# Small start loads on SyncE's queue, two expert passes per accumulation, and a rearranged end in a mixture-of-experts decoder layer

## The chip, the cores and the metric

The kernel runs on one core of one Trainium2 chip. The metric is the device time of one execution in microseconds (us); lower is better. Times come from repeated executions of the same program, and one further execution was profiled.

## What is computed

One decoder layer over 512 tokens of width 1024, all in float32: a mixer (four mLSTM heads and eight sliding-window attention heads), a normalisation, a hierarchical mixture of experts, and a second normalisation. Cut to what matters here:

```
p = x @ W_in                                  # 2824 columns, conv + silu on the first 1024
y = W_out [ mLSTM_heads(p) ; SWA_sink_heads(p) ]
x = LN1(alpha * x + y)
g   = argmax(x @ w_group_router + b_group_router)          # one of 4 groups
e   = top-2 of the 8 experts of group g                    # two weights per token
out = sum over the token's two experts of  weight * (silu(x @ gate[e]) * (x @ up[e])) @ down[e]
x = LN2(alpha * x + out)
```

There are 32 experts; gate, up and down of one expert are 1 MiB each, so the experts' weights are 96 MiB, and every one is read once.

## The kernel before, in words

**Start.** Tokens stand in four chunks of 128. SyncE's queue (SP) loads the transposed input in four pieces (`xc`, L159) and `W_in` in column groups (`wraw`, L153; group 0 in thirds). ScalarE (ACT) rounds each piece to a high part (`xh`, `wh`, L185), VectorE (DVE), and for a few pieces GpSimd (POOL), subtracts it to get the low part (`xl`, `wl`, L186), and TensorE (PE) multiplies high by high, low by high and high by low (L234, L235, L239). Before its first real product PE runs ten warm-up products (L654). Group 0 is done for chunks 0 to 3, then groups 1 and 2; their results are copied out of PSUM at L258 to L264 (`tq`, `gates`). The small inputs (gate bias, attention sinks, rope tables cos and sin, conv weights and bias, the mLSTM norm's weights, the two router biases) are loaded through POOL's queue (L167, L686 to L701). POOL also builds the masks and then turns queries and keys (`rope`, L330 to L340).

**Queue order.** SP, PE and DVE run in the order in which the kernel is written wherever `manual_schedule` names them; elsewhere, for ACT and POOL, a scheduler chooses. In the built program each transfer of SP also waits until the one eight places ahead of it has landed, so at most eight are under way.

**Experts.** Thirteen passes (`NP = 13`), their kinds in `ORDER = "BBBCABABABBCC"`. A pass of kind A or B serves two experts, one of kind C four, over 128 gathered rows of tokens. Pass p: POOL gathers the rows (`xg`, L1000), PE transposes them (L1012), `gu_part` multiplies by gate and up in four quarters of 2 of 8 K blocks (L1044; a quarter needs the weights of all experts of the pass, quarters 0 and 1 the first half of each, 2 and 3 the second), `pair_h` makes silu(gate) * up (ACT L1059, DVE L1060), `dn_t` transposes it (PE L1067, DVE copy L1069), `pass_dn` multiplies by down (L1077). `y_split` scales the result and splits it into `yh` (ACT, L1087) and `yl` (DVE, L1088); `back_hot` makes a 0/1 matrix `oh` of the tokens (L1096); and `add_back` brings the result back to the tokens: for every chunk c and half u one accumulation in PSUM, `oh` times `yh` and `oh` times `yl` (L1113), added by DVE to the running rows `x1` (L1115; the first time L1118). In the loop over p the quarters of pass p stand between the pieces of the `add_back` of pass p - 2, the transposes and the down product of pass p - 1. Passes 0 and 1 share one accumulation, every later pass has its own.

Weights lie in 16 ring slots of 1 MiB; `prefetch` issues a load on SP as soon as a slot is free, in the order pass, then first half of gate and up, second half, down (for the last pass the second half of down comes at the very end).

**The end.** After the loop: broadcast rows of the last norm (`l2_fill`, L1461), a matrix of rows that belong to the same token (`same_rows`, L1471), `add_back` of pass 10, down product and `add_back` of pass 11, the norm of every chunk (`norm_s` statistics on DVE L1527, with small steps on POOL L194 to L1531; `norm_i` on ACT L1539; `norm_z` times weight on DVE L1543; `norm_o` plus bias L1546, three halves of eight on POOL and five on DVE; `norm_d` output on SP L1549). Then pass 12 (kind C): quarters 0 and 1 (`last_gu(0)`), `base_rows` of all four chunks (L1562, the running rows of the tokens that this pass serves), quarters 2 and 3 (`last_gu(1)`), `pair_h`, `dn_t`, down, a scaled copy (ACT, DVE L1604), a product with `same` (L1606), a norm of those rows (L1611, L1613) and one scatter over the output (POOL, L1614). A loop over further rows follows; it runs only when experts overflow.

```python
            if prev:
                py = pass_dn(hts[0], p - 1)
                parts = later([(back(p - 1), y_split(py, cws[:, p - 1:p], *y_slots()))])
```

Of the kernel before, what the change touches and what calls it, by code (L numbers as in the profile page):

```python
# [23 lines left out]
NCH = 4  # L24
P = 128
# [47 lines left out]
def ap_of(src, offset, dims):  # L73
    return bass.AP(tensor=src.tensor, offset=src.offset + offset, ap=dims)
# [3 lines left out]
def layer_kernel(ctx, tc, x, w_in, conv_w, conv_b, gate_bias, norm_w, sinks, w_out, ln1_w, ln1_b,  # L78
# [84 lines left out]

    ident = C.tile([P, P], F32, name="ident")
    make_identity(nc, ident)
    def bload(t, src, n):
        G.dma_start(t, ap_of(src, 0, [[0, P], [1, n]]))  # L167
        return t

    gbias = bload(C.tile([P, 8], F32, name="gbias"), gate_bias, 8)  # L170


    def some(g, n):
# [509 lines left out]
        return u  # L683

    sink = bload(C.tile([P, 8], F32, name="sink"), sinks, 8)
    G.dma_start(cosd, cos_t.rearrange("(c p) d -> p c d", p=P))  # L686
    G.dma_start(sind, sin_t.rearrange("(c p) d -> p c d", p=P))
    cw = C.tile([P, 4, 8], F32, name="cw")
    G.dma_start(cw, ap_of(conv_w, 0, [[32, P], [8, 4], [1, 8]]))
    cb = C.tile([P, 8], F32, name="cb")  # L690
    G.dma_start(cb, ap_of(conv_b, 0, [[8, P], [1, 8]]))
    triu = tri("triu", 1, OP.is_ge)
    ktri = tri("ktri", -1, OP.is_ge, I32)
    negm = tri("negm", 1, OP.is_ge, BF16, val=0.0, fill=-1e30)
# [2 lines left out]
    G.tensor_scalar(nw, nw, 0.5, None, op0=OP.mult)  # L697
    rb = C.tile([1, 40], F32, name="rb")
    G.memset(rb, -1e30)
    G.dma_start(rb[:, 0:4], ap_of(b_gr, 0, [[0, 1], [1, 4]]))  # L700
    G.dma_start(rb[:, 8:40], ap_of(b_er, 0, [[0, 1], [1, 32]]))  # L701
    mhalf = C.tile([P, 4], F32, name="mhalf")
    G.memset(mhalf, -0.5)
    iot = C.tile([P, 2 * P], F32, name="iot")
# [358 lines left out]
    def dn_t(h):  # L1063
        ph = bank("ph", tag="t")[:, 0:256].rearrange("p (j n) -> p j n", j=2)
        hv = h.rearrange("p (q j) -> p j q", j=2)
        for j in range(2):
            TE.transpose(ph[:, j], hv[:, j], ident)  # L1067
        ht = W.tile([P, DE], F32, name="ht", bufs=1).rearrange("p (j n) -> p j n", j=2)
        V.tensor_copy(ht, ph)  # L1069
        return ht  # L1070
# [10 lines left out]
    def pass_dn(ht, p):  # L1081
        return dn_mm(ht, pairs[p], TILES[ORDER[p]])

    def y_split(py, cs, yh, yl):
        for u in range(2):
            us = slice(512 * u, 512 * u + 512)
            A.activation(yh[:, us], py[u], AF.Copy, scale=cs)  # L1087
            V.scalar_tensor_tensor(yl[:, us], py[u], cs, yh[:, us], op0=OP.mult, op1=OP.subtract)  # L1088
        return yh, yl

    def y_slots():
        return [slot(n, F32R)[:, :DM] for n in ("yh", "yl")]
# [12 lines left out]
    def add_back(oys, cs=range(NCH)):  # L1105
        mm = [(o, t) for o, y in oys for t in y]
        for c in cs:
            for u in range(2):
                us = slice(512 * u, 512 * u + 512)
                xu = x1[c][:, us]  # L1110
                b = bank("cb", tag="pj")
                for i, (o, t) in enumerate(mm):
                    TE.matmul(b, o[:, c * P:(c + 1) * P], t[:, us], start=i == 0, stop=i == len(mm) - 1)  # L1113
                if (c, u) in scaled:
                    V.tensor_add(xu, xu, b)  # L1115
                else:
                    scaled.add((c, u))
                    V.scalar_tensor_tensor(xu, xu, ALPHA, b, op0=OP.mult, op1=OP.add)  # L1118
# [334 lines left out]
    def l2_fill(i):  # L1453
        d, w = l2d
        t = slot("l2")[:, :DM]
        l2.append(t)
        for u in range(2):
            g = 2 * i + u
            p_ = bank("l2")
            for s in range(2):  # L1460
                TE.matmul(p_, w[:, g:g + 1].to_broadcast([16, P]), d[:, s].rearrange("p k n -> p (k n)"),  # L1461
                          start=s == 0, stop=s == 1)
            A.copy(t[:, 512 * u:512 * u + 512], p_)


    def same_rows(p):
        t = slot("same")
        m, w = t[:, 0:P], t[:, P:2 * P + 2]
        tk = tok2[0][:, p:p + 1]
        b = bank("same", tag="t")  # L1470
        TE.matmul(b[:, 0:P], tk.to_broadcast([P, P]), ident, start=True, stop=True)  # L1471
        V.tensor_scalar(m, b[:, 0:P], tk, None, op0=OP.is_equal)
        V.scalar_tensor_tensor(w[:, 0:P], triu, 0.5, m, op0=OP.is_lt, op1=OP.mult)
        V.tensor_reduce(w[:, P:P + 1], w[:, 0:P], axis=AX.X, op=OP.add)
        V.tensor_scalar(w[:, P + 1:P + 2], tk, 0.0, None, op0=OP.is_lt)
        V.tensor_add(w[:, P:P + 1], w[:, P:P + 1], w[:, P + 1:P + 2])
        V.scalar_tensor_tensor(row[:, 0:1], w[:, P:P + 1], BIG, tk, op0=OP.mult, op1=OP.add)
        return m

    def back(p):  # L1480
        return back_hot(slot("oh2", F32R)[:, 0:T], toks(p))


    def later(oys):
        return [lambda c=c: add_back(oys, (c,)) for c in range(NCH)]

    with tc.manual_schedule(engines={ENG.PE, ENG.DVE}):
        parts = later([(back(p), y_split(pys[p], cws[:, p:p + 1], *y_slots())) for p in range(2)])
        for p in range(2, NP - 1):
            release(p, False)  # L1490
            if p > 2:
                release(p - 1, True)
            prefetch(99)
            hts = []
            pg = pass_gu(xs, p % 2, p, (lambda: hts.append(dn_t(prev))) if prev else None, parts)
            h = pair_h(pg)
            if parts:
                parts[3]()
                parts = ()
            if p == 8:  # L1500
                ob = hots(NP - 1)
            if p == NP - 3:
                l2d = l2_parts()
            if p % 2:
                xs = pairs_g(hn)
                if p + 3 < NP:
                    hn = fetch(p + 3)
            if prev:
                py = pass_dn(hts[0], p - 1)
                parts = later([(back(p - 1), y_split(py, cws[:, p - 1:p], *y_slots()))])  # L1510
                if p == NP - 2:
                    ht = dn_t(h)
            prev = h
        for i in range(2):
            l2_fill(i)
        sm = same_rows(NP - 1)
        for f in parts:
            f()
        o = back(NP - 2)

    HS = [slice(0, 512), slice(512, 1024)]
# [26 lines left out]
    def norm_d(c):  # L1548
        SP.dma_start(o2[c * P:(c + 1) * P], zo.pop(c))  # L1549
# [7 lines left out]
    with tc.manual_schedule(engines=MAN):  # L1557
        zr = [bank("zr", tag=t) for t in ("t", "m")]

        def base_rows(c):  # L1560
            for h in range(2):
                TE.matmul(zr[h], ob[:, c, 0:P], x1[c][:, HS[h]], start=c == 0, stop=False)  # L1562

        def last_gu(u):
            for g in range(2):
                gu_part(pg, xs, 0, pairs[p], TILES[ORDER[p]], 2 * u + g)

        y = y_split(pass_dn(ht, p - 1), cws[:, p - 1:p], *y_slots())
        add_back([(o, y)], (0, 1))
        norm_s(0, base(0))  # L1570
        add_back([(o, y)], (2,))
        norm_i(0)
        norm_s(1, base(1))
        add_back([(o, y)], (3,))
        norm_i(1)
        norm_z(0)
        norm_s(2, base(2))
        norm_o(0, 0, G)
        norm_z(1)
        norm_i(2)  # L1580
        norm_s(3, base(3))
        norm_o(1, 0, G)
        norm_o(0, 1, V)
        norm_z(2)
        norm_i(3)
        norm_o(2, 0, G)
        norm_o(1, 1, V)
        norm_z(3)
        norm_o(2, 1, V)
        norm_o(3, 0, V)  # L1590
        norm_o(3, 1, V)
        for c in range(NCH):
            norm_d(c)
        pg = bank("pg")
        last_gu(0)
        for c in range(NCH):
            base_rows(c)
        last_gu(1)
        h = pair_h(pg)
        ht = dn_t(h)  # L1600
        py = pass_dn(ht, p)
        held_y = slot("yf")[:, :DM]
        A.activation(held_y[:, HS[0]], py[0], AF.Copy, scale=cws[:, p:p + 1])
        V.tensor_scalar(held_y[:, HS[1]], py[1], cws[:, p:p + 1], None, op0=OP.mult)  # L1604
        for h in range(2):
            TE.matmul(zr[h], sm, held_y[:, HS[h]], start=False, stop=True)  # L1606
        norm_s(4, zr)
        mv = mvs[4]
        z = slot("z")[:, :DM]
        for h, hs in enumerate(HS):  # L1610
            V.scalar_tensor_tensor(z[:, hs], zr[h], mv[:, 0:1], l2[0][:, hs], op0=OP.subtract, op1=OP.mult)  # L1611
        for h, hs in enumerate(HS):
            V.scalar_tensor_tensor(z[:, hs], z[:, hs], mv[:, 2:3], l2[1][:, hs], op0=OP.mult, op1=OP.add)  # L1613
        G.indirect_dma_start(out=o2[:, :], out_offset=bass.IndirectOffsetOnAxis(ap=row[:, 0:1], axis=0),  # L1614
                             in_=z, in_offset=None, bounds_check=T - 1, oob_is_err=False)
# [118 lines left out]
```

## Time and profile before

| | |
|---|---|
| median of 3 runs | 511.06 us (509.45 to 511.36) |
| profiled execution | 507.21 us; span from first to last instruction 505.5 us, 1.71 us lie around it |
| PE busy | 477.5 us, 94% of the span |
| DVE busy | 301.4 us, 60% |
| ACT, POOL busy | 149.9 us, 30%; 107.7 us, 21% |
| moved by DMA | 133.14 MB, mean 263 GB/s |
| mean granted TensorE clock | 0.986 |

A busy PE is one that holds a matmul, not one at its peak. The share of an engine over the whole span says little here: the start waits for its first loads, the middle computes, and from about 230 us on the experts' weights stream in. So a stretch is read by the waits that end last in it.

### The profile page before, as it was taken

The numbers are of one execution on the slowest core, as the hardware profiler recorded it, in microseconds if no ns is written. First come the engines' busy times: TensorE is split into PE (matmuls) and PEld (weight loads), VectorE is DVE, ScalarE is ACT, GpSimd is POOL, SyncE is SP. The second block draws the span as 40 slices with busy tenths as digits, with TensorE's granted clock in tenths as the row PEclk, the third lists the DMA queues.
The fourth block names the chain that finished last, engine by engine and source line by source line (L and its number), as shares of the span: only waits on it lengthen the run. The fifth ranks groups of instructions, "written<-read, shape, count | busy, mean of one in ns | idle before, by whom it ended". The sixth has DMA issues, their size and how long they took to land. (4 is left out here: it accounts for less than half of the span.)

```text
span 505.5 us, 8207 instructions
## 1 busy us (share of the span) xinstructions
PE 477.5 (94%) x2912; PEld 313.2 (62%) x2912; DVE 301.4 (60%) x680; ACT 149.9 (30%) x340; POOL 107.7 (21%) x142
## 2 busy tenths in 40 slices
PE   6999899999999999999999999999999999899980
PEld 6999688879898987788865443334343344253320
DVE  3553788894358766778771533545554655357953
ACT  4552555787434261011310202012111120131320
POOL 8099804412230110102003101001000000100531
PEclk8999989999999999999999999999999999999996
DMA  8523212220892654509988999999999999999740
GB/s 263 200 99 124 72 41 84 83 85 2 291 393 57 176 208 131 174 28 379 404 285 323 376 416 395 413 414 412 412 412 413 414 412 409 415 409 409 312 167 21
DMA packets 35324, 133.14 MB, mean 263 GB/s; under 512 B 6138, under 2 KB 6170, under 8 KB 31952
## 3 DMA queue, kind: packets, MB, share of 16 engines
q1 hardware_dynamic: 33184, 126.04, 65.5%
q0 software_dynamic: 2096, 6.54, 3.7%
q8 instruction: 24, 0.39, 0.3%
q14 instruction: 20, 0.16, 0.1%
HBM read 128.16 MB, written 4.72 MB: 263 GB/s over the span
## 5 line engine op out<-in xcount | busy, mean ns | idle before, releaser
L1044 PE MATMUL pg<-we,xs 128*32 128x512 f32 (+1 forms) x608 | 100.5, 599 | 2.2 <-DMA we<-in_w_exp_up 2.2
L234 PE MATMUL pj<-wh,xh 128*128 128x256 f32 (+1 forms) x224 | 64.6, 290 | 2.6 <-ACT wh L185 2.6
L1115 DVE TENSOR_TENSOR x<-x,cb 128x512 f32<-128x512 f32 x80 | 51.3, 682 | 23.7 <-PE cb L1113 23.3
L235 PE MATMUL pj<-wh,xl 128*128 128x256 f32 (+1 forms) x224 | 63.9, 287 | 0.5 <-DVE xl L186 0.5
L1044 PEld LDWEIGHTS pg<-we,xs 128*32 128x32 f32 (+1 forms) x608 | 26.5, 119 | 54.6 <-issue 49.3
L239 PE MATMUL pj<-wl,xh 128*128 128x256 f32 x192 | 53.3, 283 | 0.0
L1077 PE MATMUL yo<-we,ht 128*32 128x512 f32 (+1 forms) x304 | 48.8, 597 | 0.5 <-DVE ht L1069 0.5
L234 PEld LDWEIGHTS pj<-wh,xh 128*128 128x128 f32 x224 | 43.5, 194 | 3.2 <-ACT wh L185 3.1
L1113 PE MATMUL cb<-yh,oh 128*128 128x512 f32 x96 | 42.6, 444 | 1.8 <-DVE x L1115 1.3
L235 PEld LDWEIGHTS pj<-wh,xl 128*128 128x128 f32 x224 | 43.6, 195 | 0.7 <-DVE xl L186 0.7
L1059 ACT ACTIVATE hid<-pg 128x256 f32<-128x256 f32 x13 | 5.0, 383 | 126.4 <-PE pg L1044 126.4
L1113 PE MATMUL cb<-yl,oh 128*128 128x512 f32 x96 | 38.0, 396 | 0.4 <-DVE yl L1088 0.4
L1113 PEld LDWEIGHTS cb<-yh,oh 128*128 128x128 f32 x96 | 18.1, 188 | 32.6 <-issue 22.5
L1000 POOL DMA_INDIRECT xg<-xd,row x11 | 10.5, 957 | 128.8 <-PE cb L1113 64.3
L239 PEld LDWEIGHTS pj<-wl,xh 128*128 128x128 f32 x192 | 36.3, 192 | 0.0
L186 DVE TENSOR_TENSOR wl<-wraw,wh 128x1024 fp32r<-128x1024 f32 x14 | 21.4, 1544 | 23.3 <-ACT wh L185 17.8
L1077 PEld LDWEIGHTS yo<-we,ht 128*32 128x32 f32 (+1 forms) x304 | 13.0, 119 | 26.8 <-issue 25.4
L1088 DVE SCALAR_TENSOR_TENSOR yl<-yo,cws,yh 128x512 fp32r<-128x512 f32 x24 | 17.7, 749 | 18.4 <-ACT yh L1087 17.4
L185 ACT ACTIVATE wh<-wraw 128x1024 fp32r<-128x1024 f32 (+2 forms) x23 | 23.2, 1021 | 14.3 <-DMA wraw<-in_w_in 4.6
L1087 ACT ACTIVATE yh<-yo,cws 128x512 fp32r<-128x512 f32 x24 | 16.4, 688 | 37.0 <-PE yo L1077 36.7
L189 PE MATMUL pj<-xh,wh 128*128 128x512 f32 x64 | 26.0, 407 | 0.0
L191 PE MATMUL pj<-xl,wh 128*128 128x512 f32 x64 | 26.0, 406 | 0.0
(339 smaller groups left out, 869.7 us busy)
## 6 DMA issues: line engine op xcount, KB each, us to landing
we<-in_w_exp_gate SPq DMA_DIRECT2D x64, 512.0 KB
we<-in_w_exp_up SPq DMA_DIRECT2D x64, 512.0 KB
we<-in_w_exp_down SPq DMA_DIRECT2D x26, 1024.0 KB
wraw<-in_w_in SPq DMA_DIRECT2D x20, 512.0 KB
we<-in_w_exp_down SPq DMA_DIRECT2D x12, 512.0 KB
xc<-in_x_columns SPq DMA_DIRECT2D x4, 512.0 KB
wo<-in_w_out SPq DMA_DIRECT2D x8, 256.0 KB
wo<-in_w_out SPq DMA_DIRECT2D x4, 512.0 KB
```

Source lines behind the costliest of these rows:

```text
L185: A.activation(hi, src, AF.Copy)
L186: eng.tensor_tensor(lo, src, hi, op=OP.subtract)
L189: TE.matmul(o, lh, rh, start=start, stop=False)
L191: TE.matmul(o, lh, rl, start=False, stop=stop)
L234: TE.matmul(o, xh[j // 2][:, j % 2, cs], ws[i][j][0], start=j == 0, stop=False)
L235: TE.matmul(o, xl[j // 2][:, j % 2, cs], ws[i][j][0], start=False, stop=False)
L239: TE.matmul(o, xh[k // 2][:, k % 2, cs], ws[i][k][1], start=False, stop=k == 7)
L1044: TE.matmul(pg[s:s + n], xs[k // 4][:, k % 4, P * b + s:P * b + s + n], ws[e][k // 4][:, :, k % 4], start=k == 0, stop=k == 7)
L1077: TE.matmul(py[u][s:s + n], ht[:, j, s:s + n], wt[e][2][j][:, 512 * u:512 * u + 512], start=j == 0, stop=j == 1)
L1088: V.scalar_tensor_tensor(yl[:, us], py[u], cs, yh[:, us], op0=OP.mult, op1=OP.subtract)
L1113: TE.matmul(b, o[:, c * P:(c + 1) * P], t[:, us], start=i == 0, stop=i == len(mm) - 1)
L1115: V.tensor_add(xu, xu, b)
```

## The change

Three edits. Small loads: all small loads but the gate bias go from POOL's queue to SP's, at the same place in the program, which is behind the loads of column group 1. The loop: the result of a pass is held until the next pass has one too, and the two are brought back in one accumulation of four products per chunk and half; `l2_fill` and `same_rows` move ahead of pass 12's transposes and the down product of pass 10. The end: the down products of passes 10 and 11 follow each other and both are brought back together; `base_rows` are spread over the quarters and the transposes of pass 12; all bias additions are on DVE; each chunk's output is issued right behind its bias; chunk 3's scaling and the outputs of chunks 2 and 3 stand behind the last `dn_t`.

```diff
-    def bload(t, src, n):
-        G.dma_start(t, ap_of(src, 0, [[0, P], [1, n]]))
+    def bload(t, src, n, eng=SP):
+        eng.dma_start(t, ap_of(src, 0, [[0, P], [1, n]]))
         return t
-    gbias = bload(C.tile([P, 8], F32, name="gbias"), gate_bias, 8)
+    gbias = bload(C.tile([P, 8], F32, name="gbias"), gate_bias, 8, G)
...
-    G.dma_start(cosd, cos_t.rearrange("(c p) d -> p c d", p=P))
-    G.dma_start(sind, sin_t.rearrange("(c p) d -> p c d", p=P))
+    SP.dma_start(cosd, cos_t.rearrange("(c p) d -> p c d", p=P))
+    SP.dma_start(sind, sin_t.rearrange("(c p) d -> p c d", p=P))
...
+    held = []
...
+            if p == NP - 2:
+                for i in range(2):
+                    l2_fill(i)
+                sm = same_rows(NP - 1)
...
                 py = pass_dn(hts[0], p - 1)
-                parts = later([(back(p - 1), y_split(py, cws[:, p - 1:p], *y_slots()))])
                 if p == NP - 2:
                     ht = dn_t(h)
+                held.append((back(p - 1), y_split(py, cws[:, p - 1:p], *y_slots())))
+                if len(held) == 2:
+                    parts, held = later(held), []
             prev = h
-        for i in range(2):
-            l2_fill(i)
-        sm = same_rows(NP - 1)
-        for f in parts:
-            f()
         o = back(NP - 2)
...
-        y = y_split(pass_dn(ht, p - 1), cws[:, p - 1:p], *y_slots())
-        add_back([(o, y)], (0, 1))
+        held.append((o, y_split(pass_dn(ht, p - 1), cws[:, p - 1:p], *y_slots())))
+        add_back(held, (0, 1))
         norm_s(0, base(0))
-        add_back([(o, y)], (2,))
+        add_back(held, (2,))
...
+        norm_out(0)
         norm_z(2)
...
+        norm_out(1)
         pg = bank("pg")
+        base_rows(0)
         last_gu(0)
-        for c in range(NCH):
-            base_rows(c)
+        base_rows(1)
         last_gu(1)
+        base_rows(2)
         h = pair_h(pg)
         ht = dn_t(h)
+        base_rows(3)
+        norm_z(3)
+        norm_out(2)
+        norm_out(3)
         py = pass_dn(ht, p)
```

`norm_out(c)` is both halves of `norm_o(c, h, V)` and `norm_d(c)`; sinks, conv weights and bias, norm weights and router biases change their queue as the rope tables do.

On SP, at the start (`xc` is the input, `wraw` column groups of `W_in`), the built programs differ so:

```order
-L153 DMA wraw<-in_w_in 128x1024 x20
+L153 DMA wraw<-in_w_in 128x1024 x2
+L167 DMA sink<-in_attn_sinks 128x8
+L686 DMA csn<-in_rope_cos 128x4x64
+L687 DMA csn<-in_rope_sin 128x4x64
+L689 DMA cw<-in_conv_w 128x32
+L691 DMA cb<-in_conv_b 128x8
+L167 DMA csa<-in_mlstm_norm_w 128x512
+L700 DMA rb<-in_b_group_router 1x4
+L701 DMA rb<-in_b_expert_router 1x32
+L153 DMA wraw<-in_w_in 128x1024 x18
```

The eight small loads now stand behind the input and column groups 0 and 1, and ahead of groups 2 and on.

On PE, from the down product of pass 10 on (`yo` 64x512 is pass 10, `yo` 32x512 pass 11, `l` the rows of the last norm, `cb` the accumulation back to the tokens), before:

```order
L1077 MATMUL yo<-we,ht 64x512 x8
L1067 MATMUL ph<-ident,hid 128x128 x2
L1461 MATMUL l_4449<-l2d,l2w 128x512 x2
L1461 MATMUL l_4453<-l2d,l2w 128x512 x2
L1461 MATMUL l_4458<-l2d,l2w 128x512 x2
L1461 MATMUL l_4462<-l2d,l2w 128x512 x2
L1471 MATMUL same<-ident,tok_2063 128x128
L1113 MATMUL cb<-yh,oh_4434 128x512
L1113 MATMUL cb<-yl,oh_4434 128x512
L1113 MATMUL cb<-yh,oh_4434 128x512
L1113 MATMUL cb<-yl,oh_4434 128x512
L1077 MATMUL yo<-we,ht 32x512 x5
```

and now:

```order
L1461 MATMUL l_4360<-l2d,l2w 128x512 x2
L1471 MATMUL same<-ident,tok_2063 128x128
L1012 MATMUL xp<-ident,xg 128x128 x8
L1077 MATMUL yo<-we,ht 64x512 x8
L1067 MATMUL ph<-ident,hid 128x128 x2
L1077 MATMUL yo<-we,ht 32x512 x16
L1113 MATMUL cb<-yh,oh_4402 128x512
L1113 MATMUL cb<-yl,oh_4402 128x512
L1113 MATMUL cb<-yh,oh_4411 128x512
L1113 MATMUL cb<-yl,oh_4411 128x512
```

Where pass 10's way back stood between the pieces of pass 11's down product, it now follows with pass 11's, four products to an accumulation.

On PE, from the last way back to the last products (`pg` gate and up of pass 12, `zr` its rows, `x_2172` to `x_2181` the four chunks), before:

```order
L1113 MATMUL cb<-yl,oh_4507 128x512
L1044 MATMUL pg<-we,xs 32x512 x16
L1562 MATMUL zr<-x_2172,ohr 128x512 x2
L1562 MATMUL zr<-x_2175,ohr 128x512 x2
L1562 MATMUL zr<-x_2178,ohr 128x512 x2
L1562 MATMUL zr<-x_2181,ohr 128x512 x2
L1044 MATMUL pg<-we,xs 32x512 x16
L1067 MATMUL ph<-ident,hid 128x128 x2
L1077 MATMUL yo<-we,ht 32x512 x16
L1606 MATMUL zr<-yf,same 128x512 x2
```

and now:

```order
L1113 MATMUL cb<-yl,oh_4411 128x512
L1565 MATMUL zr<-x_2172,ohr 128x512 x2
L1044 MATMUL pg<-we,xs 32x512 x16
L1565 MATMUL zr<-x_2175,ohr 128x512 x2
L1044 MATMUL pg<-we,xs 32x512 x16
L1565 MATMUL zr<-x_2178,ohr 128x512 x2
L1067 MATMUL ph<-ident,hid 128x128 x2
L1565 MATMUL zr<-x_2181,ohr 128x512 x2
L1077 MATMUL yo<-we,ht 32x512 x16
L1611 MATMUL zr<-yf,same 128x512 x2
```

The same products, with one chunk's rows before each half of gate and up, one before the transposes and one behind them.

On ACT the scheduler, which is free there at the start, also moved something: the two `wh` of column group 2 (L185), which stood behind the copy of group 1's chunk 0 (L261), now stand behind the copies of chunks 0 to 2.

## Rows read from the trace of the kernel before

**Rows 1.** Windows: us, busy PE, PEld, DVE, ACT, POOL (instructions), PEclk, DMA share, GB/s

```profile
350.00:375.00 25.00, 25.00 (x131) 9.68 (x130) 12.25 (x22) 2.14 (x4) 0.00 (x0) 1.00 1.02 412
...
476.00:480.00 4.00, 4.00 (x11) 1.72 (x10) 3.90 (x7) 1.52 (x2) 3.65 (x6) 1.00 0.35 137
```

**Rows 2.** Timeline, PE, passes 10 and 11: start, length, what, [idle before <-releaser]

```profile
440.62 1.88 PE L1044 MATMUL pg<-we,xs 128*32 128x512 f32 x10 [2.21 <-DMA we<-in_w_exp_up]
...
443.24 0.40 PE L1113 MATMUL cb<-yh,oh 128*128 128x512 f32 x1
...
443.48 0.39 PE L1113 MATMUL cb<-yl,oh 128*128 128x512 f32 x1
...
443.80 1.92 PE L1044 MATMUL pg<-we,xs 128*32 128x512 f32 x16
...
447.65 3.65 PE L1077 MATMUL yo<-we,ht 128*64 128x512 f32 x16
...
451.67 2.19 PE L1461 MATMUL l<-l2d,l2w 16*128 16x512 f32 x8
```

**Rows 3.** Timeline, PE, the last stage

```profile
471.16 3.64 PE L1044 MATMUL pg<-we,xs 128*32 128x512 f32 x32
...
474.73 7.13 PE L1562 MATMUL zr<-x,ohr 128*128 128x512 f32 x16
...
481.80 3.64 PE L1044 MATMUL pg<-we,xs 128*32 128x512 f32 x32
...
487.11 0.50 PE L1067 MATMUL ph<-ident,hid 128*128 128x128 f32 x2 [1.67 <-DVE hid L1060]
...
488.13 3.64 PE L1077 MATMUL yo<-we,ht 128*32 128x512 f32 x32 [0.52 <-DVE ht L1069]
```

**Rows 4.** Timeline, DVE and POOL, the last stage

```profile
463.68 1.40 DVE L1088 SCALAR_TENSOR_TENSOR yl<-yo,cws,yh 128x512 fp32r<-128x512 f32 x2
...
465.02 1.34 DVE L1115 TENSOR_TENSOR x<-x,cb 128x512 f32<-128x512 f32 x2
...
467.78 1.28 DVE L1527 BATCH_NORM_STATS2 lnst<-x 128x6 f32<-128x512 f32 x2
...
481.40 2.97 POOL L1546 TENSOR_TENSOR z<-z,l 128x512 f32<-128x512 f32 x2
...
482.32 2.60 DVE L1543 TENSOR_TENSOR z<-z,l 128x512 f32<-128x512 f32 x2 [1.02 <-ACT z L1539]
...
486.65 0.41 DVE L1060 TENSOR_TENSOR hid<-hid,pg 128x256 f32<-128x256 f32 x1
```

**Rows 5.** Page, costliest groups: count | busy us, mean ns | idle before, releaser

```profile
L1115 DVE TENSOR_TENSOR x<-x,cb 128x512 f32<-128x512 f32 x80 | 51.3, 682 | 23.7 <-PE cb L1113 23.3
...
L1113 PE MATMUL cb<-yh,oh 128*128 128x512 f32 x96 | 42.6, 444 | 1.8 <-DVE x L1115 1.3
```

**Rows 6.** Timeline, ACT and PE, the first loads

```profile
9.28 0.86 ACT L185 ACTIVATE wh<-wraw 128x792 fp32r<-128x792 f32 x1 [2.58 <-DMA wraw<-in_w_in]
...
10.20 0.59 PE L234 MATMUL pj<-wh,xh 128*128 128x264 f32 x1 [2.23 <-ACT wh L185]
...
11.57 1.34 ACT L185 ACTIVATE xh<-xc 128x256 fp32r<-128x256 f32 x4 [0.59 <-DMA xc<-in_x_columns]
```

**Rows 7.** Windows of the start (columns as in rows 1)

```profile
5.50:9.50 4.00, 1.59 (x8) 0.93 (x6) 1.74 (x3) 1.42 (x4) 3.70 (x12) 1.00 0.95 265
9.50:13.00 3.50, 2.80 (x12) 2.81 (x13) 2.83 (x6) 2.82 (x7) 3.30 (x8) 0.54 1.03 405
```

**Rows 8.** DMA queues from 5.2 to 9.3 us: packets, MB, share of the 16 engines

```profile
q1 hardware_dynamic: 365, 1.00, 65.4%
q0 software_dynamic: 77, 0.02, 24.5%
```

**Rows 9.** Timeline, ACT and DVE, column groups 1 and 2

```profile
31.43 0.37 ACT L261 COPY tq<-pj 128x256 f32<-128x256 f32 x1 [2.51 <-PE pj L239]
...
33.84 2.32 DVE L186 TENSOR_TENSOR wl<-wraw,wh 128x1024 fp32r<-128x1024 f32 x1 [3.51 <-ACT wh L185]
```

More of the change, by code (lines that the diff above doesn't have):

```diff
@@ L685, in layer_kernel @@
     sink = bload(C.tile([P, 8], F32, name="sink"), sinks, 8)
-    G.dma_start(cosd, cos_t.rearrange("(c p) d -> p c d", p=P))
-    G.dma_start(sind, sin_t.rearrange("(c p) d -> p c d", p=P))
+    SP.dma_start(cosd, cos_t.rearrange("(c p) d -> p c d", p=P))
+    SP.dma_start(sind, sin_t.rearrange("(c p) d -> p c d", p=P))
     cw = C.tile([P, 4, 8], F32, name="cw")
-    G.dma_start(cw, ap_of(conv_w, 0, [[32, P], [8, 4], [1, 8]]))
+    SP.dma_start(cw, ap_of(conv_w, 0, [[32, P], [8, 4], [1, 8]]))
     cb = C.tile([P, 8], F32, name="cb")
-    G.dma_start(cb, ap_of(conv_b, 0, [[8, P], [1, 8]]))
+    SP.dma_start(cb, ap_of(conv_b, 0, [[8, P], [1, 8]]))
     triu = tri("triu", 1, OP.is_ge)
@@ L699, in layer_kernel @@
     G.memset(rb, -1e30)
-    G.dma_start(rb[:, 0:4], ap_of(b_gr, 0, [[0, 1], [1, 4]]))
-    G.dma_start(rb[:, 8:40], ap_of(b_er, 0, [[0, 1], [1, 32]]))
+    SP.dma_start(rb[:, 0:4], ap_of(b_gr, 0, [[0, 1], [1, 4]]))
+    SP.dma_start(rb[:, 8:40], ap_of(b_er, 0, [[0, 1], [1, 32]]))
     mhalf = C.tile([P, 4], F32, name="mhalf")
@@ L1566, in last_gu @@
                 gu_part(pg, xs, 0, pairs[p], TILES[ORDER[p]], 2 * u + g)
-        y = y_split(pass_dn(ht, p - 1), cws[:, p - 1:p], *y_slots())
-        add_back([(o, y)], (0, 1))
+        held.append((o, y_split(pass_dn(ht, p - 1), cws[:, p - 1:p], *y_slots())))
+        add_back(held, (0, 1))
         norm_s(0, base(0))
-        add_back([(o, y)], (2,))
+        add_back(held, (2,))
         norm_i(0)
         norm_s(1, base(1))
-        add_back([(o, y)], (3,))
+        add_back(held, (3,))
         norm_i(1)
@@ L1577, in layer_kernel, with norm_out @@
         norm_s(2, base(2))
-        norm_o(0, 0, G)
+        norm_i(2)
         norm_z(1)
-        norm_i(2)
         norm_s(3, base(3))
-        norm_o(1, 0, G)
-        norm_o(0, 1, V)
-        norm_z(2)
[L1585 to L1591, printed above, removed]
-        for c in range(NCH):
-            norm_d(c)
+        norm_i(3)
+        def norm_out(c):
+            for h in range(2):
+                norm_o(c, h, V)
+            norm_d(c)
+        norm_out(0)
+        norm_z(2)
+        norm_out(1)
         pg = bank("pg")
+        base_rows(0)
         last_gu(0)
-        for c in range(NCH):
-            base_rows(c)
+        base_rows(1)
         last_gu(1)
+        base_rows(2)
         h = pair_h(pg)
         ht = dn_t(h)
+        base_rows(3)
+        norm_z(3)
+        norm_out(2)
+        norm_out(3)
         py = pass_dn(ht, p)
```

## The prediction

> **What bounds the kernel now.** I read the windows first, for the stretch in which the experts' weights stream: from 350 to 375 us the 16 DMA engines are busy for a share of 1.02 and move 412 GB/s, and PE is busy all of the time [rows 1]. Both look full, so the timeline has to say which one waits. In pass 11 PE stops once, for 2.21 us, at 440.62, for the second half of that pass's weights [rows 2]. So up to there the stream sets the pace, and work that PE or DVE saves before 440.62 comes back as a longer stop there. Behind it the stream is no longer what is late: from 476 to 480 only 137 GB/s move [rows 1], so all weights are in by about 479, while pass 12's down product, their last user, starts at 488.13 [rows 3]. From 440.62 to the end the order of PE's products and DVE's steps counts. The third view is the start: PE has waited 2.23 us at 10.20 for the second third of column group 0, which ACT got only at 9.28 after 2.58 us of its own wait for DMA [rows 6]. What PE does later follows on it (groups of products behind each other, weight slots freed by them), so time won at 10 us shifts the stream and the end with it.
>
> **The loop.** Ten separate ways back of passes 2 to 11 become five of twice the products. That removes 40 of the 80 additions of 0.682 us, 27.3 us of DVE. I cost this at nothing: DVE is the one that waits there (23.3 of its 23.7 idle us before these are for PE), and PE's products waited 1.3 us in all for such an addition [rows 5]. The products stay as many. An odd pass is now longer by 4 x 4 products at 0.24 us (443.24 to 443.48 [rows 2]), 3.8 us, the even one before it shorter by as much; PE is then never behind where it was, slots come free no later, and the stop of 2.21 us takes up what is left. If that cover were gone, pass 11 would run late by up to 3.8 - 2.2 = 1.6 us.
>
> **From 440.62 on, step by step.** In all of this I keep the moment of the stop.
> - Third quarter, transposes, four products, last quarter at 443.80 [rows 2]; now four products more, 4 x 0.24 = 0.96, so 444.76.
> - Before, 3.85 us from there to pass 10's down product at 447.65 [rows 2]. Now 0.96 more for the second set of four, 2.19 for the rows of the last norm, and some 0.25 for the same-token product; pass 10's down product starts at 452.0 and ends after 3.65 at 455.65.
> - Pass 11's transposes and the copy of their result: 1.02 from 487.11 to 488.13 in pass 12 [rows 3], so its down product runs from 456.7 to 460.4. It shares PSUM banks with pass 10's result, which ACT and DVE must have split first; I add 0.5: 460.9.
> - Before, pass 11's down product stood in pieces between pass 10's way back; its split on DVE began at 463.68 and the first addition came at 465.02 [rows 4]. Now the split's halves (1.40 for two) follow the down product's, and the first addition comes at about 460.9 + 0.4 + 1.4 = 462.7. From there the chain is DVE's, as before: two additions (1.34), statistics (1.28) per chunk; every half chunk waits for two more products before DVE has it, which costs about 0.5 until the first chunks are through. The last way back ended at 471.16 [rows 3]; now at 471.16 - 2.3 + 0.8 = 469.7.
> - Then the same products as before: two halves of gate and up, 2 x 3.64, four chunks' rows, 7.13 [rows 3], and now the transposes (0.50) between them. Before, PE had nothing but the transposes from 481.80 + 3.64 = 485.44 to 488.13, while silu, the multiplication (486.65 [rows 4]) and the transposes went round; now chunk 2's rows cover silu, chunk 3's the copy. With 0.4 of gaps: 469.7 + 7.28 + 7.13 + 0.5 + 0.4 = 485.0 for the down product that started at 488.13. **The end gains 3.1 us.**
> - What follows, scaled copy to scatter, is unchanged if DVE is free. Behind the transposes it has now six halves (chunk 3 times weight, chunks 2 and 3 plus bias) of 0.64 (half of 1.28 for two [rows 4]), 3.8 us, beside a down product of 3.64: hidden, with nothing to spare. The last outputs now go out behind these halves, still ahead of the whole norm of pass 12's rows that the scatter comes after.
>
> Bounds for this part: with no gain before 471.16, only the hidden turn-round is left, 471.16 + 15.3 = 486.5, a gain of 1.7. With the whole 3 us ahead of the additions kept, 4.6. The weights allow more, so they set no end.
>
> **The start.** The eight small loads leave POOL's queue, and SP takes them up behind column group 1. From 5.5 to 9.5 the engines were busy for a share of 0.95 but moved 265 GB/s, where 405 are moved right behind [rows 7]. In that time POOL's queue had 77 packets with 0.02 MB and held 24.5% of the engines' time [rows 8]. Tiny transfers thus took a quarter of the engines and the big ones got the rest. The gate bias stays on POOL, so not all of it goes. At 405 the window's bytes take 4.0 x 265/405 = 2.6, so 1.4 us less. PE also ran from 9.5 to 13, after its wait, at a granted clock of 0.54, that is mostly at 1.2 of its 2.4 GHz [rows 7]; at the full clock that stretch would be 1.6 shorter. I take 1.0 of it, since PE soon needs the next input piece (11.57 [rows 6]), which comes earlier by the 1.4 too: 2.4 together. Bounds: 0, if the big loads are slow for another reason, and 1.4 + 1.6 = 3.0.
>
> Here a rule speaks against the change. The Trainium skill (DMA: Bandwidth & Descriptors, Issuing engines are not separate DMA queues) says that transfers from any issuing engine end on the same 16 DMA engines, and that another issuer only saves its own issue time. By it alone the move is worth nothing and the sum ends 2.4 us higher, case A below. The trace agrees that the queues share the engines [rows 8]; my gain comes from the place behind column group 1, not from the queue.
>
> Against it stands ACT's new order: the split of group 2 now starts behind the copy of chunk 2, at 31.43 [rows 9]. High part (0.86 in [rows 6], for less data), then low part at up to 2.32 (33.84 [rows 9]) make some 3.4 us; PE takes 2.51 + 0.37 = 2.9 for the chunk between [rows 9]. It may find the split late by 0 to 1.5, for the second half too; I take 0.5. The small loads themselves are first read in the rope step, long behind their landing, and cost nothing. **The start gains 1.9 us.**
>
> **Sum.** 1.9 + 3.1 = 5.0. The profiled execution took 507.21 (span 505.5 and 1.71 around it) and would take 502.2. It lies 3.85 below the median of 511.06, so on the scale of the runs I take the same 5.0 off: **506.1 us**.
>
> **Rivals.**
> - A, the start gives nothing, by the rule above or because the gate bias alone does the harm: 3.1 less 0.2 for ACT's order, 508.2. For it: the gate bias is the first of POOL's loads. Against it: 24.5% of the engines over 4 us is more than one tiny load should hold. Chance 0.20.
> - B, the additions start no earlier, since DVE has both passes' splits and `oh` ahead of them: 1.7 + 1.9 = 3.6, 507.5. Chance 0.15.
> - C, **slower**: DVE becomes the bound of the end. From 466 on it has four statistics and two pairs of additions (8.7 us), then ten halves of norm work ahead of pass 12's multiplication, which PE needs by 482.8. At 0.64 each that is 481.1. Two such cost 2.60 while POOL added beside them (481.40 and 482.32 [rows 4]); at that price, 1.30 each, it is 487.7, and the six halves before the scaled copy cost another 4: 8.1 worse than my sum, 3.1 slower than before, 514.2. It decides from 0.8 us a half. Against it: the change takes POOL's additions out. Chance 0.05.
> - D, both parts at their upper ends, 3.0 + 4.6 = 7.6: 503.5. Chance 0.10.
>
> **How the numbers follow.** My forecast has 0.50. The range is 502.5 to 510.8: D's end and 1 us more below, as all D's bounds are soft, above it both parts at their lower ends (1.7, less a full 1.5 at the start); C and some of D and A lie outside. A difference of 0.5%, 2.6 us, is about what a measurement of this kernel can tell from none; faster means below 508.5. Of my forecast 0.42 lies there, of A 0.10, of B 0.09, all of D: 0.71. Same: 0.08 + 0.10 + 0.05 = 0.23. Slower: C and the tail of B, 0.06.
>
> **What the profile would show.** Right: ACT gets the second third of column group 0 at about 7 us and no half clock follows, or a shorter one; half the L1115 additions; a stop for DMA in pass 11 still, some 2 us earlier; pass 12's down product 5 us earlier; its transposes right behind chunk 2's rows. Wrong: ACT still waits until 9 us (A), the last way back still ends 30.5 us behind the stop (B), the multiplication or the scaled copy waits in DVE's queue while PE stands (C).

## The result

The changed kernel took a median of 502.28 us, the kernel before 511.06 (five runs each); the ratio is 0.9856, with a 95% interval of 0.9809 to 0.9903. A second comparison, of 12 and 35 runs, gave 503.9 against 508.59, ratio 0.9926 (0.9896 to 0.9956). The ratios leave out runs in a slower state, such as the first profiled execution of the changed kernel (508.11 us at a mean granted clock of 0.970), and are not the quotients of the medians named. So the change is faster, by 0.7 to 1.4%, where 1.0% was forecast (5.0 of 511.06). The kernel before against itself gave 0.9994 (0.9958 to 1.0030). I read the profile of the changed kernel from the second occasion: 501.64 us, span 499.9.

Much of the scatter goes with TensorE's granted clock, whose mean is listed for every run. Over the 198 runs of the second comparison and of all experiments, fitted with one slope for every kernel, the time falls by 3.9 us for each 0.01 of clock. At equal clock the change is then worth 3.7 us (3.0 to 4.3). This is an estimate.

The page's groups for the way back, the stage that adds a pass's result to the tokens (`x` and `cb`; columns as in [rows 5]), show half the additions and as many products:

```profile
L1115 DVE TENSOR_TENSOR x<-x,cb 128x512 f32<-128x512 f32 x40 | 27.2, 685 | 26.3 <-PE cb L1113 26.3
L1113 PE MATMUL cb<-yh,oh 128*128 128x512 f32 x96 | 40.3, 420 | 0.8 <-DVE x L1115 0.8
```

The start, that answers to [rows 6] and [rows 7]: the timeline (ACT's second third of column group 0, PE behind it), then the windows.

```profile
9.59 0.86 ACT L185 ACTIVATE wh<-wraw 128x792 fp32r<-128x792 f32 x1 [2.88 <-DMA wraw<-in_w_in]
10.50 0.59 PE L234 MATMUL pj<-wh,xh 128*128 128x264 f32 x1 [2.53 <-ACT wh L185]
```

```profile
5.50:9.50 4.00, 1.28 (x7) 0.85 (x6) 1.75 (x3) 1.21 (x3) 3.58 (x13) 0.89 0.96 284
9.50:13.00 3.50, 2.50 (x11) 2.50 (x12) 2.52 (x5) 3.04 (x7) 0.43 (x2) 0.50 1.03 418
```

Nothing is won here: the second third comes at 9.59 (9.28 before), PE waits 2.53 (2.23), and the half clock follows as before. Between 13 and 56 us, where ACT's new order could have made PE wait, PE is busy all of the time:

```profile
13.00:56.00 43.00, 43.00 (x316) 41.36 (x315) 19.30 (x32) 17.70 (x38) 27.98 (x31) 0.97 0.40 127
```

PE's timeline from the stop on (PE's wait for DMA in pass 11), that answers to [rows 2] and [rows 3]:

```profile
437.96 1.88 PE L1044 MATMUL pg<-we,xs 128*32 128x512 f32 x10 [1.54 <-DMA we<-in_w_exp_up]
...
445.96 2.12 PE L1461 MATMUL l<-l2d,l2w 16*128 16x512 f32 x8
448.00 0.49 PE L1471 MATMUL same<-ident,tok 128*128 128x128 f32 x2
448.33 1.72 PE L1012 MATMUL xp<-ident,xg 128*128 128x128 f32 x8
449.98 4.79 PE L1077 MATMUL yo<-we,ht 128*64 128x512 f32 x16
...
455.72 3.64 PE L1077 MATMUL yo<-we,ht 128*32 128x512 f32 x32 [0.52 <-DVE ht L1069]
...
468.44 1.88 PE L1565 MATMUL zr<-x,ohr 128*128 128x512 f32 x4
...
483.16 3.64 PE L1077 MATMUL yo<-we,ht 128*32 128x512 f32 x32
```

From the end of the stop to pass 12's down product it is 483.16 - 437.96 = 45.20, before 488.13 - 440.62 = 47.51. PE has no wait left between chunk 0's `base_rows` (468.44) and that product. But pass 10's down product takes 4.79, not 3.65, and pass 12's transposes 1.72, not 1.04: the granted clock fell there, from full to half.

On DVE, the steps around pass 12's transposes:

```profile
481.55 0.42 DVE L1069 COPY ht<-ph 128x256 f32<-128x256 f32 x1 [0.93 <-PE ph L1067]
481.89 1.28 DVE L1546 TENSOR_TENSOR z<-z,l 128x512 f32<-128x512 f32 x2
483.09 2.49 DVE L1549 TENSOR_TENSOR z<-z,l 128x512 f32<-128x512 f32 x4
486.87 0.75 DVE L1609 TENSOR_SCALAR yf<-yo,cws 128x512 f32<-128x512 f32 x1 [1.29 <-PE yo L1077]
```

The six halves that were put behind the copy are done at 485.58, and DVE then waits 1.29 for the down product.

### The profile page after: what moved, and what is told of

It is laid out like the page before. It is cut to its first block, busy times and chain, and to the rows that moved or that the text cites. A ratio compares the mean times of both kernels' runs of the same rounds, so it can differ in the third digit from the quotient of the medians.

```text
span 506.4 us, 8113 instructions
## 1 busy us (share of the span) xinstructions
PE 480.3 (95%) x2912; PEld 322.0 (64%) x2912; DVE 277.1 (55%) x643; ACT 149.7 (30%) x340; POOL 98.3 (19%) x131
## 5 line engine op out<-in xcount | busy, mean ns | idle before, releaser
L1044 PE MATMUL pg<-we,xs 128*32 128x512 f32 (+1 forms) x608 | 102.0, 598 | 3.1 <-DMA we<-in_w_exp_up 3.0
L1044 PEld LDWEIGHTS pg<-we,xs 128*32 128x32 f32 (+1 forms) x608 | 27.8, 119 | 59.4 <-issue 53.5
L1059 ACT ACTIVATE hid<-pg 128x256 f32<-128x256 f32 x13 | 5.0, 382 | 125.2 <-PE pg L1044 125.2
L1115 DVE TENSOR_TENSOR x<-x,cb 128x512 f32<-128x512 f32 x40 | 27.2, 685 | 26.9 <-PE cb L1113 26.8
L1113 PE MATMUL cb<-yh,oh 128*128 128x512 f32 x96 | 40.3, 420 | 0.8 <-DVE x L1115 0.8
L186 DVE TENSOR_TENSOR wl<-wraw,wh 128x1024 fp32r<-128x1024 f32 x14 | 20.7, 1499 | 25.1 <-ACT wh L185 24.5
L1069 DVE COPY ht<-ph 128x256 f32<-128x256 f32 x13 | 5.5, 425 | 44.4 <-PE ph L1067 44.4
L1088 DVE SCALAR_TENSOR_TENSOR yl<-yo,cws,yh 128x512 fp32r<-128x512 f32 x24 | 17.7, 749 | 17.4 <-ACT yh L1087 16.4
L185 ACT ACTIVATE wh<-wraw 128x1024 fp32r<-128x1024 f32 (+2 forms) x23 | 23.1, 1021 | 12.6 <-DMA wraw<-in_w_in 4.2
L190 PE MATMUL pj<-xh,wl 128*128 128x512 f32 x64 | 25.8, 403 | 0.0
## 6 DMA issues: line engine op xcount, KB each, us to landing
we<-in_w_exp_gate SPq DMA_DIRECT2D x64, 512.0 KB, 11.4
```

What stands on the lines that cost most here:

```text
L185: A.activation(hi, src, AF.Copy)
L186: eng.tensor_tensor(lo, src, hi, op=OP.subtract)
L190: TE.matmul(o, ll, rh, start=False, stop=False)
L1044: TE.matmul(pg[s:s + n], xs[k // 4][:, k % 4, P * b + s:P * b + s + n], ws[e][k // 4][:, :, k % 4], start=k == 0, stop=k == 7)
```

## The start: whose small loads hold up the first weights

First, eight loads moved and nothing else: the kernel before with the changed kernel's lines for `bload`, cos, sin, `cw`, `cb`, `rb`.

> The kernel before with the small loads alone on SP (gate bias on POOL). My forecast: ACT gets the second third of column group 0 at about 7 us and the time is 1.9 us shorter. Theory 'start gives nothing': ACT gets it at 9.3 as before, the half clock from 9.5 to 13 stays, and the time is that of before within 1 us.

Measured: 508.08 against 508.59, ratio 0.9995 (0.9961 to 1.0029). ACT's row for the second third:

```profile
10.59 0.86 ACT L185 ACTIVATE wh<-wraw 128x792 fp32r<-128x792 f32 x1 [3.85 <-DMA wraw<-in_w_in]
```

The move of the eight gives nothing. The reverse, the changed kernel with the eight back on POOL:

> The changed kernel with the small loads back on POOL's queue: loop and end alone. My forecast: 1.9 us slower than the changed kernel. Theory 'start gives nothing': the same as the changed kernel within 1 us, so about 7 us faster than before.

Measured: 505.08, ratio 0.9941 (0.9909 to 0.9972), beside 0.9926 for the changed kernel: the same within the intervals. So no gain is seen from moving eight, and what the change gains lies in the loop and the end.

Then the ninth load:

```diff
-    gbias = bload(C.tile([P, 8], F32, name="gbias"), gate_bias, 8, G)
+    gbias = bload(C.tile([P, 8], F32, name="gbias"), gate_bias, 8)
```

> The changed kernel with the gate bias on SP too, behind the input pieces, so that POOL's queue holds no transfer in the first 9 us. Theory 'tiny transfers' (my forecast's, the gate bias being what is left of it): ACT gets the second third of column group 0 at about 7 us and 1 to 2 us are gained. Theory 'the big loads are slow by themselves': ACT gets it at 9.3 again, 5.5 to 9.5 us moves 260 to 280 GB/s again, and the time stays within 1 us of the changed kernel.

Measured: 497.85 against 508.22, ratio 0.9792 (0.9755 to 0.9829), the fastest kernel of the study. ACT's row and the windows:

```profile
7.74 0.86 ACT L185 ACTIVATE wh<-wraw 128x792 fp32r<-128x792 f32 x1 [1.03 <-DMA wraw<-in_w_in]
```

```profile
5.50:9.50 4.00, 2.10 (x12) 1.63 (x12) 2.79 (x4) 2.92 (x6) 2.87 (x11) 1.00 0.96 353
9.50:13.00 3.50, 3.38 (x27) 3.17 (x26) 2.58 (x8) 1.58 (x5) 0.00 (x0) 1.00 1.03 403
```

The engines moved 353 GB/s where it was 284, at the same share of busy time, and the clock is full behind it. Is it the gate bias, or that POOL's queue is empty? Two more variants of the kernel before: all nine loads on SP, and the gate bias alone (`SP.dma_start(gbias, ...)` at L171, the other eight on POOL).

> The kernel before with all nine small loads on SP, loop and end as before. Moving eight of them gave -0.1 us, moving the ninth, the gate bias, on top of the changed kernel made it 6 us shorter (503.9 to 497.85). Theory 'POOL's queue at the start': the ninth gives the same here, second third at 7.7, no half clock from 9.5 to 13, about 6 us less than before (502.2). Rival 'only together with the new end': it needs the rearranged end, less than 2 us here.

Measured: 506.77 against 509.53, ratio 0.9940 (0.9897 to 0.9982).

```profile
7.01 0.86 ACT L185 ACTIVATE wh<-wraw 128x792 fp32r<-128x792 f32 x1 [0.28 <-DMA wraw<-in_w_in]
```

> The kernel before with the gate bias alone on SP, behind the input pieces; the other eight stay on POOL. Theory 'any transfer of POOL among the first loads': the sinks, conv weights and biases still come from POOL before 5 us, so ACT gets the second third at 9.3 and the time is that of before within 1 us. Rival 'the gate bias alone does the harm': about 6 us less than before, as when all nine are moved.

Measured: 508.46, ratio 0.9971 (0.9936 to 1.0005). The first and the second third:

```profile
6.81 0.86 ACT L186 ACTIVATE wh<-wraw 128x792 fp32r<-128x792 f32 x1 [2.26 <-DMA wraw<-in_w_in]
...
9.49 0.86 ACT L186 ACTIVATE wh<-wraw 128x792 fp32r<-128x792 f32 x1 [1.20 <-DMA wraw<-in_w_in]
```

So neither eight nor one is enough. In the nine profiles of kernels with POOL's gate bias, alone or with the other eight, ACT got the second third at 9.01 to 10.59, and at 9.49 where only the other eight came from POOL; in the three with all nine on SP, at 7.01 to 7.74. Moving all nine is worth 0.6% with the old end, 2.8 between the medians (by the interval 0.9 to 5.2). That rules out the 6 us of the first theory as this part's own gain; the rival's 'less than 2' it doesn't rule out.

A stretch of single profiles says more. Up to PE's first `sc` product (L372) the edits of all these kernels differ only in these loads. That product, and ACT's first silu, in pass 0 (L1059), first of the kernel before, then with the gate bias on SP:

```profile
62.99 0.55 PE L372 MATMUL sc<-kT,qs 128*128 128x128 f32 x3 [2.44 <-DVE qs L354]
...
260.27 0.38 ACT L1059 ACTIVATE hid<-pg 128x256 f32<-128x256 f32 x1 [6.87 <-PE pg L1044]
```

```profile
60.60 0.55 PE L372 MATMUL sc<-kT,qs 128*128 128x128 f32 x3 [2.43 <-DVE qs L354]
...
257.89 0.38 ACT L1059 ACTIVATE hid<-pg 128x256 f32<-128x256 f32 x1 [6.87 <-PE pg L1044]
```

That is 2.4 us earlier at both; in these two profiles the clock falls once in between, near 64 us. The `sc` product comes at 62.99 to 65.53 in the ten profiles with loads from POOL, and at 60.60 to 61.45 in the three with all nine on SP, 1.5 us earlier at the least.

Last, is it POOL's queue, or any tiny load among the first big ones? The changed kernel with `eng` = ACT for the gate bias:

> The changed kernel with the gate bias issued by ACT, ahead of its first work, so at about 1 us as early as POOL issued it, but not from POOL's queue. Theory 'POOL's queue': as fast as with the gate bias on SP, 497.9 within 1 us, second third at 7.7. Rival 'any tiny transfer among the first big ones': it holds the big ones up from there too, second third at about 9.3, time of the changed kernel, 503 to 504.

Measured: 505.47 against 509.53, ratio 0.9886 (0.9832 to 0.9941), which does not differ from the changed kernel's 0.9926.

```profile
7.57 0.86 ACT L185 ACTIVATE wh<-wraw 128x792 fp32r<-128x792 f32 x1 [0.70 <-DMA wraw<-in_w_in]
...
8.96 0.85 ACT L185 ACTIVATE wh<-wraw 128x792 fp32r<-128x792 f32 x1
```

Here the first third is late (7.57 instead of 5.2): ACT issued at 0.78, with SP's first load (0.79). The second third follows closely, and the first `sc` product comes at 62.30. Up to 5.3 us the engines moved 0.56 MB, with the gate bias on SP 1.13 MB. So it isn't POOL's queue alone: 4 KB in 128 rows hold the first big loads up from ACT's queue too, and they don't from SP's, behind the input pieces. Whether the queue decides or the moment is not shown: POOL issued the gate bias at 1.37 and ACT at 0.78, but SP only at 4.1, and no run issued it late from POOL or first from SP.

## The loop and the stream: where the stop for weights stands

The stop ends 2.66 us earlier in the changed kernel (437.96), though nothing was won at the start. Does the pairing bring the weights earlier? The kernel before, with passes 2 to 9 in pairs and pass 10 and the end as they were:

```diff
...
-                parts = later([(back(p - 1), y_split(py, cws[:, p - 1:p], *y_slots()))])
+                held.append((back(p - 1), y_split(py, cws[:, p - 1:p], *y_slots())))
+                if len(held) == 2 or p == NP - 2:
+                    parts, held = later(held), []
```

> The kernel before with passes 2 to 9 brought back in pairs, pass 10 and the end as before. My forecast and theory 'end only': no gain, the stop for weights in pass 11 takes up what PE saves, time of before within 1 us, stop's end at 440.6. Theory 'stream': 1.5 to 3 us faster, the stop's end at 438 to 439.

Measured: 512.98 against 508.59, ratio 1.0071 (1.0036 to 1.0106): slower, which neither theory had. PE's timeline, in a profiled execution of 517.54 us:

```profile
445.17 3.27 PE L1044 MATMUL pg<-we,xs 128*32 128x512 f32 x10 [2.07 <-DMA we<-in_w_exp_up]
...
463.44 3.15 PE L1077 MATMUL yo<-we,ht 128*32 128x512 f32 x10
...
481.42 4.42 PE L1044 MATMUL pg<-we,xs 128*32 128x512 f32 x32
```

Behind the stop stand eight more products than before (pass 8's come with pass 9's), 8 x 0.24 = 1.9 us. The clock fell as well: in these three rows the same products took 1.88, 1.90 and 3.64 in the kernel before. But this execution lies 4.6 above the median, and the clock falls differently from run to run, so the rows do not size the loss. At equal clock, by the same fit, it is 2.5 us (1.9 to 3.2), so most of it is the 1.9. Pairing alone, in this form, gains nothing.

The kernel before once more, for the stream:

> The kernel before once more, for a second profile of it: from the first weight load at 298.5 (the 35th of the stream) to the down loads of pass 11 at 431.0 the first profile took 132.5 us, the kernel with the small loads moved and the loop as before took 131.0, the changed one 130.3. Theory 'stream' (the pairing lets weights come earlier): 132.5 again within 0.4. Theory 'the stream scatters': 130.5 to 131.5, and what seemed gained ahead of the stop is scatter.

The issues on SP's queue that begin and end the count (the 35th load and the first down load of pass 11), and PE's stop and pass 12's down product:

```profile
301.20 0.34 SPq L587 DMA_DIRECT2D we<-in_w_exp_gate  x1
...
432.11 0.33 SPq L593 DMA_DIRECT2D we<-in_w_exp_down  x1
```

```profile
441.17 1.88 PE L1044 MATMUL pg<-we,xs 128*32 128x512 f32 x10 [0.67 <-DMA we<-in_w_exp_up]
...
488.72 3.64 PE L1077 MATMUL yo<-we,ht 128*32 128x512 f32 x32 [0.52 <-DVE ht L1069]
```

130.9 us, where the first profile had 132.5. The five profiles with the loop of before that show both loads have 132.5, 130.9, 131.0, 130.4 and 130.8, the eight with all passes in pairs 129.9 to 131.2: that scatters by as much as it seemed to gain. The end of the stop scatters more. In the changed kernel's first profile it came at 444.38, later than before, where the second has 437.96:

```profile
444.38 1.88 PE L1044 MATMUL pg<-we,xs 128*32 128x512 f32 x10 [1.51 <-DMA we<-in_w_exp_up]
```

From the stop on, 488.72 - 441.17 = 47.55 is the 47.51 of [rows 2, 3] again. This stretch is what can be compared between single profiles, to a tenth of a microsecond.

## The end

> The changed kernel as it is, for a profile at full clock, to be read stage by stage: silu of pass 0 (260.27 before), end of the stop for DMA in pass 11 (440.62), last way back (471.16), pass 12's down product (488.13), span end (505.5). My forecast: stop 1.9 us earlier, at 438.7, and pass 12's down product at 483.1. Theory 'end only': the stop stays at 440.6 within 0.5, and all of the gain, 5 us or more, lies between the stop and pass 12's down product. Theory 'stream': silu of pass 0 stays, and the stop comes 1.5 to 3 us earlier, since half of the loop's additions are gone.

The stretch from the stop to pass 12's down product shrank by 2.3, less than 'end only' had it; that the stop moved is scatter, as shown above. The profile of the changed kernel with the loads on POOL shows the same end at full clock:

```profile
438.98 1.88 PE L1044 MATMUL pg<-we,xs 128*32 128x512 f32 x10 [1.61 <-DMA we<-in_w_exp_up]
...
449.36 1.26 PE L1012 MATMUL xp<-ident,xg 128*128 128x128 f32 x8
450.55 3.65 PE L1077 MATMUL yo<-we,ht 128*64 128x512 f32 x16
...
455.16 3.64 PE L1077 MATMUL yo<-we,ht 128*32 128x512 f32 x32 [0.52 <-DVE ht L1069]
...
467.89 1.88 PE L1565 MATMUL zr<-x,ohr 128*128 128x512 f32 x4
...
482.61 3.64 PE L1077 MATMUL yo<-we,ht 128*32 128x512 f32 x32
```

482.61 - 438.98 = 43.63, **3.9 less than before**; the gate bias on SP gave 43.67. The fit at equal clock has 3.7 for the whole kernel. Of the 3.9, 1.6 lie ahead of the end of the last way back (467.89 - 438.98 = 28.91, before 30.54), the rest behind it. DVE's first addition of the last way back stands 21.30 behind the stop, before 24.40 [rows 2, 4]:

```profile
460.28 1.40 DVE L1115 TENSOR_TENSOR x<-x,cb 128x512 f32<-128x512 f32 x2
```

With the fall of the clock the stretch is 45.20 to 45.29 in three profiles (the changed kernel twice, and with ACT's load). The same stretch, 449 to 453, in the windows, first of the changed kernel, then of this one:

```profile
449.00:453.00 4.00, 4.00 (x14) 1.67 (x16) 1.56 (x6) 0.55 (x1) 0.00 (x0) 0.59 1.03 412
```

```profile
449.00:453.00 4.00, 3.99 (x23) 2.02 (x24) 1.92 (x7) 1.39 (x3) 0.00 (x0) 1.00 1.03 408
```

What PE does before the fall is `l2_fill` (products of 16 rows), `same` and transposes. So I moved the first two, from ahead of pass 12's transposes to the place behind `ht = dn_t(h)`:

> The changed kernel with l2_fill and same_rows behind pass 11's transposes (between the down products of passes 10 and 11) instead of ahead of pass 12's gathered transposes. Theory 'l2 and the clock': in the changed kernel the granted clock falls to 0.50 to 0.59 right behind these eight products of 16 rows and the transposes (449 to 453), which makes pass 10's down product 4.79 instead of 3.65 and the transposes 1.72 instead of 1.04; in the new place the long products follow at full clock and cover the 0.52 that PE waits for the copy of pass 11's transposes: 1.5 to 2.3 us faster than the changed kernel. Theory 'chance': the clock falls where it will; only the 0.52 wait is covered, 0.5 us faster or the same.

Measured: 504.55 against 508.22, ratio 0.9920 (0.9890 to 0.9950); the changed kernel has 0.9926.

```profile
457.19 1.19 PE L1461 MATMUL l<-l2d,l2w 16*128 16x512 f32 x4
458.59 1.21 PE L1461 MATMUL l<-l2d,l2w 16*128 16x512 f32 x4 [0.21 <-ACT l L1463]
...
460.15 5.28 PE L1077 MATMUL yo<-we,ht 128*32 128x512 f32 x32
```

The 0.52 is covered, and the fall went along: it is pass 11's down product now that takes 5.28 instead of 3.64. The fall stands behind `l2_fill` again; the new place doesn't avoid it.

Next the `base_rows`, all four between the halves of gate and up again:

```diff
-        base_rows(0)
         last_gu(0)
-        base_rows(1)
+        for c in range(NCH):
+            base_rows(c)
         last_gu(1)
-        base_rows(2)
...
-        base_rows(3)
```

> The changed kernel with the four base_rows together between the two halves of gate and up, as before. My step 'the turn-round is hidden': PE again stands while silu, the multiplication and the copy of the transposes go round (1.67 and 0.52 of waits in the kernel before), so pass 12's down product comes 1.5 to 2.5 us later and the kernel is that much slower than the changed one. Rival 'DVE bounds the end': its queue is as late either way, no difference within 1 us.

Measured: 504.96 against 508.22, ratio 0.9899 (0.9862 to 0.9937), which can't be told from the changed kernel's. The timeline from the last way back on can:

```profile
472.52 3.64 PE L1044 MATMUL pg<-we,xs 128*32 128x512 f32 x32
476.10 7.13 PE L1565 MATMUL zr<-x,ohr 128*128 128x512 f32 x16
483.16 3.64 PE L1044 MATMUL pg<-we,xs 128*32 128x512 f32 x32
487.79 0.51 PE L1067 MATMUL ph<-ident,hid 128*128 128x128 f32 x2 [0.99 <-DVE hid L1060]
488.81 3.64 PE L1077 MATMUL yo<-we,ht 128*32 128x512 f32 x32 [0.52 <-DVE ht L1069]
```

488.81 - 472.52 = 16.29; spread out it is 482.61 - 467.89 = 14.72 (483.16 - 468.44 is 14.72 too), before it was 16.97. So spreading them takes out 1.57, nearly all of it the two waits, 0.99 and 0.52. The other 0.7 is the wait ahead of the transposes, 0.99 where it was 1.67: DVE's bias additions no longer stand ahead of the multiplication that PE waits for.

Both good parts together, the gate bias on SP and `l2_fill` behind pass 11's transposes:

> The changed kernel with the gate bias on SP and with l2_fill and same_rows behind pass 11's transposes. The new place covers the 0.52 that PE waits there, and leaves the 0.2 that l2_fill then waits for ACT: 0.3 to 0.6 us less than 497.85. If the granted clock falls there, as it did in the same place at the late start, 1.6 us more than that.

Measured: 502.33 against 509.53, ratio 0.9847 (0.9793 to 0.9901): faster than the kernel before, but not shown to be better than the gate bias alone. Its profile has the fall behind `l2_fill` again, and one more at 240 to 248.

## Why the prediction was right, and where it was not

- **The sum.** 5.0 was forecast; the two comparisons give 7.4 (1 - 0.9856 of 511.06) and 3.8 (1 - 0.9926 of 508.59). Sign and size hold, the terms don't: the 1.9 of the start did not come, and the end gave 3.9 where 3.1 was forecast. So the total is right in part by luck. So are two of the signs: pass 12's down product came 4.97 earlier (483.16 for 488.13), but 2.66 of that is where the stop fell, which came early without any gain at the start and 3.76 late in the first profile.
- **The start: wrong.** 1.9 forecast, nothing measured. The step that failed is "the gate bias stays on POOL, so not all of it goes": I took the harm to shrink with the share of time that POOL's queue holds. That share is no steady number: for the same stretch it is 24.5% in the first profile of the kernel before [rows 8] and 9.8% in the second, 3.2% and 17.4% in two of the changed kernel, and the big loads were late in all of them. Where all nine go, the second third comes at 7.0 to 7.7 and the gain is of the size of my upper bound (3.0; measured 2.8 by the medians, 2.4 in the two profiles above). Rival A had the start right. Its total of 2.9 lies in the interval of the second comparison (2.2 to 5.3), but below that of the first (4.96 to 9.76); 5.0 lies in both. Of A's two reasons the gate bias alone does the harm only as long as no other is left. The other is the rule of the Trainium skill (DMA: Bandwidth & Descriptors, Issuing engines are not separate DMA queues) that another issuer only saves its own issue time. It agrees with the runs that moved eight or one. Moving all nine did gain, but it changed the queue and the moment together, so it does not decide about the rule.
- **ACT's new order**, 0.5 of loss: nothing. PE has no wait between 13 and 56 us.
- **The loop at nothing: right.** Half the additions are gone from DVE, which waited for PE anyway, and pairing alone gained nothing.
- **The end: right in its steps.** Counted from the stop, forecast and measured at full clock (in the profile with the loads back on POOL): pass 10's down product 11.4 and 11.57, pass 11's 16.1 and 16.18, the last way back 29.1 and 28.91, pass 12's down product 44.4 and 43.63. The first three are within 0.2, and the additions did start earlier, so B is out. B's sign, 30.5 for the last way back, does stand in the changed kernel's profile (30.48), but there the fall of the clock makes it. The last term was undersized: I put 0.4 of gaps and 0.5 of transposes into it; there are no gaps, and chunk 3's rows follow the transposes after 0.23 (481.12 to 481.35).
- **Not in the sum:** the fall of the clock behind `l2_fill`, which took 1.6 to 1.7 back in six of the eight profiles with the new end.
- **DVE at the end (C): out.** Its halves took 0.64 (1.28 for two at 481.89), not 1.30. The six behind the copy end 1.29 before DVE's next step can start; I had them "with nothing to spare".
- **Sums that don't close,** though nothing hangs on them: without the start's 2.4 the sum is 508.5, where A has 508.2; C's 4.9 (487.7 less 482.8) and 4 make 8.9, not 8.1; and the step to 469.7 adds 0.8 where the sentence before it gives 0.5.

## What to carry to other kernels

In the first microseconds a small load issued early from another queue than the first big loads can cost about as much as a rearranged stage saves: here moving all of them behind the input in the big loads' own queue gained, and moving all but one gained nothing. Work taken from an engine that waits is worth nothing where it is taken; of the 3.9 at the end, 1.6 came where PE's own products were put into its waits and 1.6 from an earlier start of the last additions. When times scatter by 1%, compare single profiles over a stretch between two events of one engine: 47.51 to 47.56 in four profiles of the old end, 43.63 and 43.67 in two of the new one.

## What the runs showed of the hardware that I had not expected

The share of busy time that a queue's packets have does not say what they cost the others: 5.5 to 9.5 us moved 262 to 303 GB/s in ten profiles with POOL's share (5.2 to 9.3 us) anywhere from 3.2% to 24.5%, and 353 to 364 in three with none. The Trainium skill (DMA: Bandwidth & Descriptors, SWDGE vs HWDGE vs iDMA) says that POOL's loads and SP's feed different queues inside each DMA engine, between which it takes turns. That would fit a few tiny packets that hold up big ones; no run here shows the turns. The gate bias on ACT's queue, which did harm too, is listed in a queue of its own (q10, SP's loads in q1).

Most of the scatter between runs goes with TensorE's clock. The kernel with the loads back on POOL took 501.89 us at a mean granted clock of 0.985 and 509.02 at 0.975. One place where it comes from is the router's small products and the products that gather rows behind them (`ohr` times `x`), here in the first profile of the kernel before and in the second:

```profile
238.00:252.00 14.00, 12.98 (x118) 12.11 (x119) 11.59 (x60) 4.53 (x16) 0.00 (x0) 1.00 1.03 405
```

```profile
238.00:252.00 14.00, 13.32 (x95) 12.97 (x96) 8.94 (x50) 3.15 (x14) 0.00 (x0) 0.76 1.03 406
```

PE is busy in both, at full clock in one and falling to half clock in the other, and the 32 gathering products there took 3.82 and 5.56. Ten of fourteen profiles fall there. With the gate bias on SP the profile shows no fall between 66 us and the end of PE's work, and its six runs lie within 497.52 and 498.69; the kernel with `l2_fill` moved as well had falls again (499.13 to 504.47, on another chip). Of the 10.4 us between its median and that of the kernel before, 3.9 lie in the stretch at the end (47.55 to 43.67) and some 2.4 at the start. Falls of the clock that its profile lacks could make the other 4; why it lacks them stays open.
